# A decoder layer on one core: linear attention's state taken per 128 tokens, seven products over whole chunks, and other buffers for the first loads

## The chip, the cores and the metric

The kernel runs on one core of one Trainium2 chip. The time is the device time of one execution in microseconds (us): the median of 3 runs was 1633.13 us (1632.35 to 1633.36). The profile is of one further execution.

## What is computed

One layer of a hybrid decoder on 256 tokens of width 2048, with 256 memory tokens, all in float32. One wide projection of the normalised input feeds three branches: gated linear attention (4 heads, key width 128, value width 256), stick-breaking attention (8 heads of 128) and cross-attention into the memory (4 heads of 256). Each branch has its own projection to 2048, the three are merged by sigmoid gates, an output projection and a residual follow, then a SwiGLU block of inner width 5632.

```python
proj = rmsnorm(x, attn_norm) @ w_in     # gq gk gv gr ga1 | sq sk sv | mq | gates
log_a = log_sigmoid(ga1 @ gla_w_a2 + gla_b_a) / 16
# linear attention, per chunk of 64 tokens, b = cumsum(log_a) inside the chunk
q_e, k_e, k_d = q*exp(b), k*exp(-b), k*exp(b_last - b)
s = where(causal, q_e @ k_e.T, 0);   o = s @ v + q_e @ S
S = S * exp(b_last) + k_d.T @ v
...
merged = g0*y_gla + g1*y_sb + g2*y_mem
x = x + merged @ w_o
gate, up = split(rmsnorm(x, ffn_norm) @ w_gate_up)
x = x + (silu(gate) * up) @ w_down
```

## The kernel before

The 256 tokens are two halves of 128 rows (index `t`). Weights arrive from HBM as loads of 4 chunks of 128 rows by 512 columns (1 MB, tiles named `raw`). A float32 product is made of three matmuls in the type fp32r: each weight half-load (2 chunks, 128x1024) is split into a high and a low part (`wh` by a cast on ACT, L148; `wl` by a subtraction on DVE, L149), the activations were split once before, and high-high, high-low and low-high are added up in PSUM. Each such matmul streams 512 columns.

`gemm` (L221 to L223) multiplies all chunks by one block of 512 columns. `sgemm` (L262 to L265) takes two blocks at once and saves products: of the first 8 chunks, `p` chunks of each group of 4 are multiplied by seven products instead of eight (the scheme of Strassen in the form of Winograd: two token halves, two groups of chunks, two blocks). The sums of activations (`sh`, `sl`; `sd` for the last projection) are made once; the sums of weights are made on DVE in place (`raw<-raw`, L277) and by accumulating transfers that POOL issues (L319, L339). What is left of the chunks goes through `rest`, eight products as usual. `sgemm` begins with product `p1` into a temporary bank, which ACT copies into the accumulator (`acc<-tmp`, L302) before `rest` adds to it. With `late=True` it postpones the products that need the sums of activations. Its `put` keeps partial results in scratch pieces (`cv`).

Work on vectors and small matmuls runs in the background: generators in a list `background`; `gemm` and `sgemm` advance the first of them by one piece at each `step()` (after each half-load of a product or of `rest`), and `flush()` runs out what is left. Within that a planner orders the instructions of each engine; each engine then runs its own in that order and waits on semaphores.

The stages in time: memory keys and values (to about 99 us), the memory queries `mq` (to 145), `sq` with memory attention in the background (to 207), `sk`, `sv` (to 293), `gqk` and `gv` with the stick-breaking heads in the background (to 394), `gr`, the two branch projections with linear attention in the background (440 to 554), gates and the third branch (to 847), the output projection `w_o` in two pairs of blocks (to 935), and the SwiGLU block in three parts. The last down projection has 12 chunks; its first pair of blocks goes through `sgemm`, the last two blocks through `gemm`, and `stored` adds them to the residual (`x2s`, L1113) and sends them out.

Linear attention (`gla`, L820 to L905) takes each 128 tokens as two chunks of 64. The scores of both chunks are one matmul per head with a mask that keeps the two 64x64 diagonal blocks; the state `S` (128x256 per head) is used and renewed for each 64 tokens, with matmuls that use half the tokens (L883: `S` with 64 columns of queries; L888: 64 rows of keys and values). These are plain float32 matmuls, which the trace shows as two passes each.

At the start there are three `raw` tiles (`ring1`), and 8 matmuls on zeros run before the first weights are there (L564).

Of the kernel before, what the change touches and what calls it, by code (L numbers as in the profile page):

```python
# [59 lines left out]
def constants():  # L60
    i, j = np.arange(P)[:, None], np.arange(P)[None, :]
    same = (i // GC) == (j // GC)
    blocks = [
        i == j,
        i < j,
        (i <= j) & same,
        i > j,
        np.ones((P, P), bool),
        (i <= j) & same,
        (i > j) & same,  # L70
        (i // GC) == np.arange(P // GC)[None, :],
    ]
    scale = [1, 1, 1, 1, 1, 1 / TAU, 1 / TAU, 1 / TAU]
    return np.concatenate([b.astype(np.float32) * np.float32(s) for b, s in zip(blocks, scale)], 1)
# [3 lines left out]
def trunk(ctx: ExitStack, tc: tile.TileContext, a, out):  # L78
# [11 lines left out]
    def widen(name, raw, w, side="right"):  # L90

        pool = tc.alloc_tile_pool(name=name, bufs=1, side=side, reuse_waits="tile")
        free_raw.extend([(pool, raw)] * raw)
        splits.extend([(pool, w)] * w)
        return pool

    def narrow(pool):

        for x in (free_raw, splits):
            x[:] = [y for y in x if y[0] is not pool]  # L100
        pool.release()
# [70 lines left out]
    def loads():  # L172

        slot = pool, bufs = free_raw.pop(0)
        return pool.tile([P, KG, NB], F32, tag="raw", name="raw", bufs=bufs), lambda: free_raw.append(slot)
# [54 lines left out]
    def sgemm(xs, forms, w, blks, p, row0=0, late=False, moved=True):  # L230
# [62 lines left out]
        def put(at, *src):  # L293

            if late or at[0]:
                c[at] = piece()
                dst = c[at][:]
            else:
                dst = o[at][:]
                begun.add(id(o[at]))  # L300
            if len(src) == 1:
                act.copy(dst, src[0][:])  # L302
            else:
                dve.tensor_tensor(dst, src[0][:], src[1][:], op=ALU.subtract)
# [184 lines left out]
    def normed_T(dst, src, heads, dim, gain, scratch):  # L489


        ss = small.tile([P, 2, heads], F32, name="hn_ss")
        for t in range(2):
            for n in range(0, MIX, NB):
                sq = scratch()
                act.activation(sq[:], src[:, t, n : n + NB], AF.Square)
                dve.tensor_reduce(
                    ss[:, t, n // dim : (n + NB) // dim],
                    sq[:].rearrange("p (h d) -> p h d", d=dim),
                    axis=AX.X,  # L500
                    op=ALU.add,
                )
            yield
        y = rsqrt_mean(ss[:].rearrange("p t h -> p (t h)"), dim, 2 * heads)
        for t in range(2):
            v = src[:, t].rearrange("p (h d) -> p h d", h=heads)
            dve.tensor_tensor(
                v, v, y[:, t * heads : (t + 1) * heads].unsqueeze(2).to_broadcast([P, heads, dim]), op=ALU.mult
            )
            yield  # L510
        yield
        e = dim // P
        for c in range(0, 8, 2 * e):
            for q in range(e):

                p = tmp()
                for i in range(2):
                    ch = c + q + i * e
                    for t in range(2):
                        transpose(p[:, i * T + t * P : i * T + (t + 1) * P], src[:, t, ch * P : (ch + 1) * P])  # L520
                d = dst[:, c + q : c + q + e + 1 : e, :]
                act.activation(d, p[:].rearrange("p (c t) -> p c t", c=2), AF.Copy, scale=gain[:, q : q + 1])
                yield
# [29 lines left out]

    mk, mkT = section("mk", "a"), chunks(section("mkT", "b")[:])
# [8 lines left out]
    for _ in range(8):  # L563
        pe.matmul(idle[:], zeros[:, :P], zeros[:], start=True, stop=True)  # L564
# [47 lines left out]
    xs = [x() for x in xs]  # L612
    mempool.release()
# [111 lines left out]
    wide(sq, O_SQ)  # L725
    flush()
    skT_sv = main.tile([P, 2, 2, MIX], F32, tag="resid", name="skT_sv")
    skT, sv_ = chunks(skT_sv[:, 0]), skT_sv[:, 1]
    sqT = chunks(section("sqT", "b")[:])
    sk = section("sk", "d")  # L730
    background.append(normed_T(sqT, sq, SH, SD, g_sqs, ra))
    wide(sk, O_SK)
    flush()
    background.append(normed_T(skT, sk, SH, SD, g_sk, ra))
# [58 lines left out]
    wide(gqk, O_GQ, 2)  # L793
    wide(gv, O_GV, 2)
# [23 lines left out]
    def gla():  # L818
        for t in range(2):
# [15 lines left out]
            b, bl, dc = tmp(), tmp(), tmp()  # L835
            for dst, w in ((b, tri), (bl, rest)):
                pe.matmul(dst[:], w, lh[:], start=True, stop=False)
                pe.matmul(dst[:], w, ll[:], start=False, stop=True)
# [5 lines left out]
            qe, ke, kd = ra(), ra(), ra()  # L844
            act.activation(qe[:], b[:], AF.Exp)
            act.activation(ke[:], b[:], AF.Exp, scale=-1.0)
            act.activation(kd[:], bl[:], AF.Exp)
# [4 lines left out]
            dve.tensor_tensor(kd[:], gqk[:, t, 512:], kd[:], op=ALU.mult)  # L852
            yield from pause(3)
            turned = []
            for src in (qe, ke):
# [3 lines left out]
                turned.append(rb()[:].rearrange("p (h t) -> p h t", h=GH))  # L859
                dve.tensor_copy(turned[-1].rearrange("p h t -> p (h t)"), p[:])  # L860
                yield from pause(2)
            qeT, keT = turned
            yield from pause(2)
            p = tmp()
            for h in range(GH):
                pe.matmul(p[:, h * P : (h + 1) * P], keT[:, h], qeT[:, h], start=True, stop=True)
            sT = ra()[:].rearrange("p (h t) -> p h t", h=GH)
            nc.gpsimd.memset(sT, 0.0)
            dve.copy_predicated(sT, causal4, p[:].rearrange("p (h t) -> p h t", h=GH))
# [3 lines left out]
            o = [tmp(), tmp()]  # L873
            ov = [o[h // 2][:, h % 2 * GDV : (h % 2 + 1) * GDV] for h in range(GH)]
            vh = [gv[:, t, h * GDV : (h + 1) * GDV] for h in range(GH)]
            for c in range(2):
                s = slice(c * GC, (c + 1) * GC)
                for h in range(GH):
                    if c == 0:

                        pe.matmul(ov[h], sT[:, h], vh[h], start=h % 2 == 0, stop=False, skip_group_check=True)
                    if (t, c) != (0, 0):
                        pe.matmul(ov[h][s], qeT[:, h, s], S[h][:], start=False, stop=c == 1, skip_group_check=True)  # L883
                if (t, c) != (1, 1):
                    d = [tmp(), tmp()]
                    for h in range(GH):
                        dh = d[h // 2][:, h % 2 * GDV : (h % 2 + 1) * GDV]
                        pe.matmul(dh, kd[s, h * GDK : (h + 1) * GDK], vh[h][s], start=True, stop=True)  # L888
                        if (t, c) == (0, 0):
                            dve.tensor_copy(S[h][:], dh)  # L890
                        else:
                            f = dec[:, 2 * h + c : 2 * h + c + 1]
                            dve.scalar_tensor_tensor(S[h][:], S[h][:], f, dh, op0=ALU.mult, op1=ALU.add)
                    yield from pause(3)
# [154 lines left out]
    for n0 in range(0, D, 2 * NB):  # L1049
# [4 lines left out]
        for j, result in sgemm(ms, sm_, a["w_o"], (n0 // NB, n0 // NB + 1), 2, late=n0 == 0):  # L1054
# [28 lines left out]
    for part in (range(0, 4), range(4, 8), range(8, NF)):  # L1083
# [25 lines left out]
        def stored(n, result, width=NB):  # L1109
            for t in range(2):  # L1110
                for c in range(0, NB, width):
                    v = x2s[t][:, n + c : n + c + width]
                    dve.tensor_tensor(v, v, result(t)[:, c : c + width], op=ALU.add)  # L1113
                    nc.sync.dma_start(out[t * P : (t + 1) * P, n + c : n + c + width], v)

        for n0 in range(0, D, 2 * NB):
            if final and n0 > 0:
                for n in (n0, n0 + NB):
                    o = gemm(fs, a["w_down"], n, row0=4 * part[0])

                    stored(n, lambda t: o[t], NB // 2 if n + NB == D else NB)
                continue
            blks = (n0 // NB, n0 // NB + 1)
            for j, result in sgemm(fs, sd, a["w_down"], blks, 4, row0=4 * part[0], moved=False):
                n = n0 + j * NB
                if final:
                    stored(n, result)
                    continue
                for t in range(2):
                    v = piece()  # L1130
                    act.copy(v[:], result(t))
                    nc.gpsimd.dma_start(x2d[:, t, n : n + NB], v[:], accum_op=ALU.add)

# [50 lines left out]
```

## Time and profile before

| | |
|---|---|
| median of 3 runs | 1633.13 us |
| the profiled execution | 1632.16 us, span 1630.4 us |
| PE (matmuls) busy | 1620.5 us, 99% |
| PEld (weight loads into PE) busy | 1325.9 us, 81% |
| DVE busy | 1331.5 us, 82% |
| ACT busy | 1028.4 us, 63% |
| POOL busy | 71.2 us, 4% |
| read from HBM | 325.09 MB |
| granted TensorE clock | 1.00 |

The span runs from the first to the last instruction; the execution's own time is 1.8 us longer. PE's busy time is made of matmuls that overlap: one lasts 0.39 us from its start to its modelled end, while the next starts earlier, so work on PE is counted here by the distance of starts.

### The profile page before, as it was taken

How to read it: one execution, taken by the hardware profiler on the slowest of the kernel's cores; microseconds unless marked ns; L12 is line 12 of the kernel's file. 1: busy time of each engine (PE TensorE's matmuls, PEld its weight loads, DVE VectorE, ACT ScalarE, POOL GpSimd, SP SyncE). 2: the span in 40 equal slices, each digit the busy share in tenths (PEclk: the TensorE clock that was granted, in tenths of full speed). 3: DMA queues.
4: the chain of work that ended last, by engine and by line, in shares of the span. 5: the costliest groups of instructions: out<-in, count | busy, mean ns of one | idle time of the engine just before them, and what ended most of it. 6: DMA issues, size and time to landing. Idle time of an engine off the chain costs nothing.

```text
span 1630.4 us, 19473 instructions
## 1 busy us (share of the span) xinstructions
PE 1620.5 (99%) x7266; PEld 1325.9 (81%) x7266; DVE 1331.5 (82%) x1526; ACT 1028.4 (63%) x1251; POOL 71.2 (4%) x93
## 2 busy tenths in 40 slices
PE   9999999999999999999999999999999999999999
PEld 6888778888877788888888888888888888888887
DVE  6867788877755788897897798988888989888994
ACT  7765576766744666666565566666666666666662
POOL 0000000000000000000000000000110000110000
PEclk9999999999999999999999999999999999999999
DMA  8795667656654888888657768687897687897682
GB/s 328 281 326 161 216 223 247 201 178 203 210 166 165 283 263 257 265 281 301 185 215 234 257 225 265 207 278 245 255 281 243 208 268 255 264 263 246 203 331 92
DMA packets 65888, 390.33 MB, mean 239 GB/s; under 512 B 7265, under 2 KB 13921, under 8 KB 21633
## 3 DMA queue, kind: packets, MB, share of 16 engines
q1 hardware_dynamic: 51344, 324.36, 53.0%
q0 software_dynamic: 11504, 61.87, 19.7%
q10 hardware_dynamic: 2944, 2.85, 0.5%
q8 instruction: 57, 0.93, 0.2%
q14 instruction: 39, 0.31, 0.1%
HBM read 325.09 MB, written 12.58 MB: 207 GB/s over the span
## 4 chain that ended last, share of the span: by engine, by line
PE 96%; DMA 1%; ACT 1%; DVE 1%; issue 0%; ACTq 0%; DVEq 0%
PE acc L262 19%; PE acc L265 19%; PE acc L264 19%; PE acc L221 6%; PE acc L222 6%; PE acc L223 6%; PE tmp L262 6%; PE tmp L265 6%; PE tmp L264 6%; PE tmp L441 2%; ACT wh L148 1%; DMA raw<-in_w_mem_kv 0%; DMA od_mem<-out 0%; DVE wl L149 0%; PE tmp L888 0%; PE tmp L883 0%
## 5 line engine op out<-in xcount | busy, mean ns | idle before, releaser
L149 DVE TENSOR_TENSOR wl<-raw,wh 128x1024 fp32r<-128x1024 f32 (+1 forms) x752 | 904.2, 1220 | 240.0 <-ACT wh L148 227.1
L148 ACT CAST wh<-raw 128x1024 fp32r<-128x1024 f32 (+1 forms) x752 | 783.0, 1052 | 455.1 <-PE acc L265 239.3
L262 PE MATMUL acc<-wh,xTh 128*128 128x512 f32 x504 | 200.6, 399 | 1.7 <-ACT acc L302 1.5
L265 PE MATMUL acc<-wh,xTl 128*128 128x512 f32 x504 | 196.6, 390 | 0.0
L264 PE MATMUL acc<-wl,xTh 128*128 128x512 f32 x504 | 196.4, 390 | 0.0
L262 PE MATMUL acc<-wh,hh 128*128 128x512 f32 x452 | 178.9, 396 | 0.0
L264 PE MATMUL acc<-wl,hh 128*128 128x512 f32 x452 | 176.2, 390 | 0.0
L265 PE MATMUL acc<-wh,hl 128*128 128x512 f32 x452 | 175.1, 390 | 0.0
L277 DVE TENSOR_TENSOR raw<-raw 128x1024 f32<-128x1024 f32 x122 | 147.9, 1220 | 0.7
L221 PE MATMUL acc<-wh,oh 128*128 128x512 f32 x320 | 127.2, 399 | 0.7 <-ACT oh L151 0.6
L222 PE MATMUL acc<-wl,oh 128*128 128x512 f32 x320 | 126.0, 394 | 0.9 <-DVE wl L149 0.9
L223 PE MATMUL acc<-wh,ol 128*128 128x512 f32 x320 | 125.8, 393 | 0.0
L262 PEld LDWEIGHTS acc<-wh,xTh 128*128 128x128 f32 x504 | 94.6, 188 | 24.0 <-ACT acc L302 4.8
L265 PEld LDWEIGHTS acc<-wh,xTl 128*128 128x128 f32 x504 | 94.6, 188 | 20.1
L264 PEld LDWEIGHTS acc<-wl,xTh 128*128 128x128 f32 x504 | 94.7, 188 | 18.8
L262 PE MATMUL tmp<-wh,sh 128*128 128x512 f32 x270 | 106.5, 394 | 0.0
L265 PE MATMUL tmp<-wh,sl 128*128 128x512 f32 x270 | 105.4, 391 | 0.0
L264 PE MATMUL tmp<-wl,sh 128*128 128x512 f32 x270 | 105.3, 390 | 0.0
L262 PEld LDWEIGHTS acc<-wh,hh 128*128 128x128 f32 x452 | 84.9, 188 | 18.7 <-ACT acc L302 1.0
L265 PEld LDWEIGHTS acc<-wh,hl 128*128 128x128 f32 x452 | 84.9, 188 | 17.8
L264 PEld LDWEIGHTS acc<-wl,hh 128*128 128x128 f32 x452 | 85.0, 188 | 16.8
L221 PEld LDWEIGHTS acc<-wh,oh 128*128 128x128 f32 x320 | 60.6, 190 | 17.1 <-issue 3.2
(311 smaller groups left out, 2368.4 us busy)
## 6 DMA issues: line engine op xcount, KB each, us to landing
raw<-in_w_gate_up SPq DMA_DIRECT2D x88, 1024.0 KB, 6.1
raw<-in_w_in SPq DMA_DIRECT2D x56, 1024.0 KB, 5.1
raw<-in_w_gate SPq DMA_DIRECT2D x48, 1024.0 KB, 7.0
raw<-raw POOLq DMA_DIRECT2D x45, 1024.0 KB, 8.0
raw<-in_w_down SPq DMA_DIRECT2D x44, 1024.0 KB, 7.3
raw<-in_w_o SPq DMA_DIRECT2D x16, 1024.0 KB, 5.8
raw<-in_w_mem_kv SPq DMA_DIRECT2D x15, 1024.0 KB, 6.0
raw<-in_w_br_mem SPq DMA_DIRECT2D x8, 1024.0 KB, 5.1
```

The source lines that it names most:

```text
L148: act.copy(hi, src)
L149: dve.tensor_tensor(lo, src, hi.bitcast(F32), op=ALU.subtract)
L221: pe.matmul(o[t][:], xh[:, s], wh[:, j], start=k == 0, stop=False)
L222: pe.matmul(o[t][:], xh[:, s], wl[:, j], start=False, stop=False)
L223: pe.matmul(o[t][:], xl[:, s], wh[:, j], start=False, stop=k == nk - 1)
L262: pe.matmul(dst[:], xh, wh, start=id(dst) not in begun, stop=False, skip_group_check=True)
L264: pe.matmul(dst[:], xh, wl, start=False, stop=False, skip_group_check=True)
L265: pe.matmul(dst[:], xl, wh, start=False, stop=last, skip_group_check=True)
L277: dve.tensor_tensor(x, x, y, op=ALU.add)
L441: pe.transpose(dst, src, ident)
```

## The change

- `sgemm` uses the seven products on all 4 chunks of a group instead of 2 in `gqk`, `gv` and both pairs of `w_o` (`p` from 2 to 4; `SP` is 4). The last pair of the last down projection goes through `sgemm` with `p=2` and an order of its own (`end`) instead of two `gemm`. There, partial results of the second token half are added to the residual at once (`base`).
- Linear attention: cumulative sums, causal mask and state are taken over 128 tokens. The state is made once (from the first 128 tokens) and used once. To keep the exponents small, queries of the second 64 tokens are held in two forms, and the scores of those columns are made a second time with 64 columns. The state's four copies go from DVE to ACT, which also makes two copies of the queries per 128 tokens.
- The first loads may also use the tiles `sh`, `sl` and `d`, which are free at that time; 10 matmuls on zeros instead of 8.
- `normed_T` idles for 3 steps before it begins in three of its uses; the queries' normalisation of stick-breaking goes into the background of `sk` without a flush ahead of it.

```diff
-        (i <= j) & same,
+        i <= j,
...
-        (i > j) & same,
+        i > j,
...
-    for _ in range(8):
+    for _ in range(10):
         pe.matmul(idle[:], zeros[:, :P], zeros[:], start=True, stop=True)
...
+    free_raw.extend([(fpool, 1, "sh"), (fpool, 1, "sl"), (sec, 1, "d")])
...
+            if base and at[0]:
+                v = base(at[1])
+                dve.tensor_tensor(v, v, src[0][:], op=ALU.add)
+                if len(src) > 1:
+                    dve.tensor_tensor(v, v, src[1][:], op=ALU.subtract)
+                return
...
+        elif end:
+            seq = [a, *l21, *r0, g, h, *l22, b, *l11, e, *l12, i, f, *r1]
...
-    background.append(normed_T(mqT, mq, MH, MD, g_mq, ra))
+    background.append(normed_T(mqT, mq, MH, MD, g_mq, ra, 3))
...
+    def q_T():
+        sqT.append(chunks(section("sqT", "b")[:]))
+        yield from normed_T(sqT[0], sq, SH, SD, g_sqs, ra, 3)
+    background.append(q_T())
+    sk = section("sk", "d")
+    wide(sk, O_SK)
     flush()
...
-    wide(gqk, O_GQ, 2)
-    wide(gv, O_GV, 2)
+    wide(gqk, O_GQ)
+    wide(gv, O_GV)
...
-            b, bl, dc = tmp(), tmp(), tmp()
-            for dst, w in ((b, tri), (bl, rest)):
+            sums = [(tri, tmp())] + ([(rest, tmp())] if t == 0 else [])
...
+            act.copy(qT[:, :, :GC], p[:, :, :GC])
+            dve.tensor_tensor(qT[:, :, GC:], p[:, :, GC:], first_64, op=ALU.mult)
+            act.copy(q2, p[:, :, GC:])
...
+                pe.matmul(p2[:, h * GC : (h + 1) * GC], keT[:, h], q2[:, h], start=True, stop=True)
...
-                    if (t, c) != (0, 0):
-                        pe.matmul(ov[h][s], qeT[:, h, s], S[h][:], start=False, stop=c == 1, skip_group_check=True)
-                if (t, c) != (1, 1):
-                        pe.matmul(dh, kd[s, h * GDK : (h + 1) * GDK], vh[h][s], start=True, stop=True)
+                if t == 1:
+                    pe.matmul(ov[h], qT[:, h], S[h][:], start=False, stop=True, skip_group_check=True)
+            if t == 0:
+                    pe.matmul(d[h], kd[:, h * GDK : (h + 1) * GDK], vh[h], start=True, stop=True)
+                    act.copy(S[h][:], d[h])
...
-        for j, result in sgemm(ms, sm_, a["w_o"], (n0 // NB, n0 // NB + 1), 2, late=n0 == 0):
+        for j, result in sgemm(ms, sm_, a["w_o"], (n0 // NB, n0 // NB + 1), SP, late=n0 == 0):
...
-            if final and n0 > 0:
-                for n in (n0, n0 + NB):
-                    o = gemm(fs, a["w_down"], n, row0=4 * part[0])
...
+            end = final and n0 + 2 * NB == D
+            base = (lambda j: x2s[1][:, n0 + j * NB : n0 + (j + 1) * NB]) if final else None
+                fs, sd, a["w_down"], blks, 2 if end else SP, row0=4 * part[0], moved=end, base=base, end=end
```

Over the whole program PE has 30 fewer matmuls of 128x512 with weights, two fewer of that size in the cumulative sums, 16 fewer float32 matmuls of 256 columns and 8 more of 64 columns. ACT has 15 more casts `wh` of 128x1024, DVE 15 more subtractions `wl` and 11 more additions `raw<-raw` of that size.

The first place is PE in linear attention, first 128 tokens (`gv` are values, `ra` masked scores or keys, `S` the state, `rb` queries or keys). Before:

```order
L866 MATMUL tmp<-rb 128x128 x4
...
L881 MATMUL tmp<-gv,ra 128x256 x4
L888 MATMUL tmp<-gv,ra 128x256 x2
...
L883 MATMUL tmp<-S_3679,rb 64x256
L883 MATMUL tmp<-S_3680,rb 64x256
L883 MATMUL tmp<-S_3681,rb 64x256
L883 MATMUL tmp<-S_3682,rb 64x256
L888 MATMUL tmp<-gv,ra 128x256 x2
```

Now:

```order
L908 MATMUL tmp<-ra,rb 128x128 x4
L910 MATMUL tmp<-rb 128x64 x4
...
L928 MATMUL tmp<-gv,ra 128x256 x4
L934 MATMUL tmp<-gv,ra 128x256 x2
...
L934 MATMUL tmp<-gv,ra 128x256 x2
```

The products with the state (L883) are gone from this half, the state's renewal is there once instead of twice, and the second scores (L910) stand right behind the first.

The second place is ACT at the change from `sq` to `sk` (`ra<-sq` squares `sq` for its normalisation, `acc<-tmp` is the copy behind `p1`, `rb<-tmp` a transposed piece of memory attention). Before:

```order
L714 ACTIVATE sq<-acc,r_x 128x512
L496 ACTIVATE ra<-sq 128x512 x2
L148 CAST wh<-raw 128x1024
L714 ACTIVATE sq<-two,r_x 128x512
L148 CAST wh<-raw 128x1024
L496 ACTIVATE ra<-sq 128x512
L302 COPY acc<-tmp 128x512
```

Now:

```order
L734 ACTIVATE sq<-two,r_x 128x512
L664 COPY out<-tmp 128x256 x2
L665 DMA od_mem<-out 128x256 x2
L714 COPY rb<-tmp 128x512
L512 ACTIVATE ra<-sq 128x512 x2
L314 COPY acc<-tmp 128x512
```

Two squares and the last copy of memory attention stand ahead of the copy behind `p1`, where a cast and a square stood; the products of that last memory head now stand on PE between `p1` and the first `rest` of `sk`.

The third place is DVE in `gqk`, from the first values of the second stick-breaking head to its last (`rb<-tmp,ra`, `ra<-tmp,ra`, `rb<-rb,cst` and `rd<-rb,rc` make what the second small matmul of a head needs, `ra<-ra,tmp` and `ra<-ra,cst` what the third needs). Before:

```order
L767 SCALAR_TENSOR_TENSOR rb<-tmp,ra 128x384
L768 SCALAR_TENSOR_TENSOR ra<-tmp,ra 128x384
L769 TENSOR_TENSOR rb<-rb,cst 128x2x128
L149 TENSOR_TENSOR wl<-raw,wh 128x1024
L149 TENSOR_TENSOR rd<-rb,rc 128x384
L149 TENSOR_TENSOR wl<-raw,wh 128x1024
L779 TENSOR_TENSOR ra<-ra,tmp 128x384
L149 TENSOR_TENSOR wl<-raw,wh 128x1024
L781 TENSOR_TENSOR ra<-ra,cst 128x2x128
L304 TENSOR_TENSOR acc<-two,tmp 128x512
```

Now:

```order
L805 TENSOR_TENSOR ra<-ra,tmp 128x384
L793 SCALAR_TENSOR_TENSOR rb<-tmp,ra 128x384
L807 TENSOR_TENSOR ra<-ra,cst 128x2x128
L794 SCALAR_TENSOR_TENSOR ra<-tmp,ra 128x384
L795 TENSOR_TENSOR rb<-rb,cst 128x2x128
L152 TENSOR_TENSOR wl<-raw,wh 128x1024
L152 TENSOR_TENSOR rd<-rb,rc 128x384
L152 TENSOR_TENSOR wl<-raw,wh 128x1024
L805 TENSOR_TENSOR ra<-ra,tmp 128x384
```

The second head's values begin before the first head's last ones. On PE, between the first and the second small matmul of the first four heads there stood 24, 30, 30 and 36 matmuls with weights; now there stand 32, 22, 18 and 31. Between the second and the third stood 29, 24, 30 and 24 where now 12, 24, 15 and 13 stand.

More of the change, by code (lines that the diff above doesn't have):

```diff
@@ L228, in gemm, with sgemm @@
         return o
-    def sgemm(xs, forms, w, blks, p, row0=0, late=False, moved=True):
+    def sgemm(xs, forms, w, blks, p, row0=0, late=False, moved=True, base=None, end=False):
         nk = len(xs)
@@ L487, in project, with normed_T @@
             evac(dst[:, :, n : n + NB], gemm(xs, w, c0 + n), rstd)
-    def normed_T(dst, src, heads, dim, gain, scratch):
+    def normed_T(dst, src, heads, dim, gain, scratch, wait=0):
+        for _ in range(wait):
+            yield
         ss = small.tile([P, 2, heads], F32, name="hn_ss")
@@ L612, in trunk @@
     xs = [x() for x in xs]
+    give_up(fpool)
+    give_up(sec)
     mempool.release()
@@ L725, in trunk @@
     wide(sq, O_SQ)
+    sqT = []
+    def q_T():
[4 more added lines that the diff above has]
+    wide(sk, O_SK)
     flush()
+    sqT = sqT[0]
     skT_sv = main.tile([P, 2, 2, MIX], F32, tag="resid", name="skT_sv")
     skT, sv_ = chunks(skT_sv[:, 0]), skT_sv[:, 1]
[L729 to L734, printed above, removed]
+    background.append(normed_T(skT, sk, SH, SD, g_sk, ra, 3))
     wide(sv_, O_SV)
@@ L834, in gla @@
             yield from pause(4)
-            b, bl, dc = tmp(), tmp(), tmp()
-            for dst, w in ((b, tri), (bl, rest)):
+            sums = [(tri, tmp())] + ([(rest, tmp())] if t == 0 else [])
+            dc = tmp()
+            for w, dst in sums:
                 pe.matmul(dst[:], w, lh[:], start=True, stop=False)
@@ L851, in gla, with turned @@
             dve.tensor_tensor(ke[:], gqk[:, t, 512:], ke[:], op=ALU.mult)
-            dve.tensor_tensor(kd[:], gqk[:, t, 512:], kd[:], op=ALU.mult)
+            if t == 0:
+                kd = ra()
+                act.activation(kd[:], sums[1][1][:], AF.Exp)
+                dve.tensor_tensor(kd[:], gqk[:, t, 512:], kd[:], op=ALU.mult)
             yield from pause(3)
-            turned = []
-            for src in (qe, ke):
+            def turned(src):
                 p = tmp()
@@ L872, in gla, with pairs_of @@
             ss = small.tile([P, GH], F32, name="g_ss")
-            o = [tmp(), tmp()]
-            ov = [o[h // 2][:, h % 2 * GDV : (h % 2 + 1) * GDV] for h in range(GH)]
             vh = [gv[:, t, h * GDV : (h + 1) * GDV] for h in range(GH)]
-            for c in range(2):
-                s = slice(c * GC, (c + 1) * GC)
-                for h in range(GH):
-                    if c == 0:
-                        pe.matmul(ov[h], sT[:, h], vh[h], start=h % 2 == 0, stop=False, skip_group_check=True)
-                    if (t, c) != (0, 0):
-                        pe.matmul(ov[h][s], qeT[:, h, s], S[h][:], start=False, stop=c == 1, skip_group_check=True)
-                if (t, c) != (1, 1):
[L885 to L894, printed above, removed]
+            def pairs_of(into):
+                return [into[h // 2][:, h % 2 * GDV : (h % 2 + 1) * GDV] for h in range(GH)]
+            ov = pairs_of([tmp(), tmp()])
+            for h in range(GH):
+                pe.matmul(ov[h], sT[:, h], vh[h], start=h % 2 == 0, stop=t == 0, skip_group_check=True)
+                if t == 1:
+                    pe.matmul(ov[h], qT[:, h], S[h][:], start=False, stop=True, skip_group_check=True)
+            if t == 0:
+                d = pairs_of([tmp(), tmp()])
+                for h in range(GH):
+                    pe.matmul(d[h], kd[:, h * GDK : (h + 1) * GDK], vh[h], start=True, stop=True)
+                    act.copy(S[h][:], d[h])
+            yield from pause(3)
             for h in range(GH):
```

64 lines of the change are left out of this document (36 added, 28 removed).

## The prediction

> **What bounds the kernel now.** I read the page first: busy times, the slices, the chain that ended last.
>
> ```profile
> PE 1620.5 (99%) x7266; PEld 1325.9 (81%) x7266; DVE 1331.5 (82%) x1526; ACT 1028.4 (63%) x1251; POOL 71.2 (4%) x93
> PEclk9999999999999999999999999999999999999999
> PE 96%; DMA 1%; ACT 1%; DVE 1%; issue 0%; ACTq 0%; DVEq 0%
> ```
>
> PE is busy throughout, at full clock in every slice, and 96% of the chain is matmuls. Busy time alone would not prove that PE is full, since a matmul's 0.39 us overlaps the next one's. So I took the timeline of the last block, where nothing else runs: the first and the last of 43 matmuls.
>
> ```profile
> 1616.60 0.39 PE L223 MATMUL acc<-wh,fl 128*128 128x512 f32 x1
> ...
> 1626.12 0.39 PE L223 MATMUL acc<-wh,fl 128*128 128x512 f32 x1
> ```
>
> 42 steps in 9.52 us: a matmul of 512 columns costs 0.2267 us of PE's time. 7266 records in 1630 us make 0.224 us each on average, so PE takes nearly the whole program at this pace. The waits of PE by releaser confirm it:
>
> ```profile
> PE acc L262 <- ACT acc L302: 1.5, 2, 1.3
> PE tmp L701 <- ACT rb L694: 1.1, 1, 1.1
> ```
>
> These are the two largest behind the first microseconds, and they are below 2 us. So the time is PE's work: a removed matmul counts, as long as DVE and ACT keep up.
>
> A page of the Trainium skill speaks against this. Perfetto Trace Analysis, Identifying the Most-Contended Engine, says that matmul occupancy is no good measure, that the share of weight loads is one, and that the engine with the highest occupancy is to be improved first. By that DVE's 82% stands above PE's 81%, and a change that takes from PE and gives to DVE would gain nothing. The measured pace disagrees: the columns set it, not the weight load of 0.19 us. I keep the reading as a rival.
>
> **Seven products on whole chunks.** For the first 8 chunks a pair of blocks needs 84 matmuls with `p=4`, 90 with `p=2`, 96 with `gemm`. Four pairs go from 90 to 84 and the last down pair from 96 to 90: 30 matmuls less, 30 x 0.2267 = **6.8 us**. All lie in stages where PE is full (the first five rows below).
>
> The price is on DVE and ACT: per pair 3 more half-loads split and 2 more additions (3 in the first pair of `w_o`).
>
> ```profile
> L149 DVE TENSOR_TENSOR wl<-raw,wh 128x1024 fp32r<-128x1024 f32 (+1 forms) x752 | 904.2, 1220 | 240.0 <-ACT wh L148 227.1
> L277 DVE TENSOR_TENSOR raw<-raw 128x1024 f32<-128x1024 f32 x122 | 147.9, 1220 | 0.7
> L148 ACT CAST wh<-raw 128x1024 fp32r<-128x1024 f32 (+1 forms) x752 | 783.0, 1052 | 455.1 <-PE acc L265 239.3
> ```
>
> 26 x 1.22 = 31.7 us more on DVE in all, 15 x 1.05 = 15.8 on ACT. Does it fit? By stage (stretch, length, then busy PE, PEld, DVE, ACT, POOL):
>
> ```profile
> 293.00:344.00 51.00, 50.98 (x239) 42.77 (x240) 40.71 (x55) 35.76 (x54) 1.75 (x2) 1.00 0.61 195
> 344.00:394.00 50.00, 49.83 (x231) 41.44 (x230) 37.67 (x46) 33.14 (x47) 1.72 (x2) 1.00 0.62 189
> 847.50:891.50 44.00, 44.00 (x203) 36.42 (x203) 33.33 (x35) 23.91 (x28) 2.30 (x3) 1.00 0.61 210
> 891.50:935.00 43.50, 43.50 (x200) 35.66 (x199) 31.88 (x38) 26.67 (x38) 3.11 (x5) 1.00 0.78 265
> 1595.00:1611.00 16.00, 16.00 (x72) 13.23 (x72) 11.56 (x12) 6.05 (x6) 0.00 (x0) 1.00 0.16 63
> ...
> 935.00:982.00 47.00, 47.00 (x216) 38.88 (x216) 45.36 (x72) 31.38 (x44) 2.51 (x4) 1.00 0.63 215
> 1564.00:1595.00 31.00, 31.00 (x142) 25.56 (x141) 30.61 (x32) 22.01 (x24) 0.88 (x1) 1.00 0.83 282
> ```
>
> `gqk` becomes 40.7 + 6.1 = 46.8 of DVE in 51.0 - 1.4 = 49.6 of PE (94%), `gv` 43.8 in 48.6, `w_o` 40.6 in 42.6 and 38.0 in 42.1. The last two rows show DVE at 97% and 99% with PE fully busy, so this load alone need not stop PE. The last down pair has room: DVE is idle for more than half of the end.
>
> What does bear on PE is the chain of the stick-breaking heads, which now share 22 steps per pair instead of 19. For the second head:
>
> ```profile
> 302.13 0.38 PE L761 MATMUL tmp<-sqT,skT_sv 128*128 128x128 f32 x2
> 302.85 0.48 ACT L763 ACTIVATE ra<-tmp 128x384 f32<-128x384 f32 x1
> 307.05 0.55 DVE L149 TENSOR_TENSOR rd<-rb,rc 128x384 fp32r<-128x384 f32 x1
> 310.31 0.22 PE L778 MATMUL tmp<-rd,cr 128*128 128x128 f32 x1
> 312.29 0.42 DVE L781 TENSOR_TENSOR ra<-ra,cst 128x256 f32<-128x256 f32 x1
> ```
>
> From the first small matmul's end (302.5) to `rd` (307.6) the chain takes 5.1 us; PE came back only at 309.9. From the second's end (310.5) to 312.7 it is 2.2 us. In the new order the shortest stretches on PE are 18 matmuls (4.1 us, plus about 0.8 for a third small matmul) and 12 (2.7 us). That is about even with the chain, where 24 matmuls (5.4 us) were the least. One split of 1.22 us at the wrong place on DVE then shows on PE, and behind a waiting small matmul all weight matmuls stand still. Bounds: nothing, to 8 heads x 1.22 = 9.8 us. Nearest are the rows above, where PE did not wait; the planner spreads the heads unevenly, and I take **+1.5 us** here and +0.5 for `w_o` and the down pair: **+2.0**.
>
> **Linear attention.** Small float32 products on PE (the timeline groups passes, two per product):
>
> ```profile
> 447.12 0.62 PE L837 MATMUL tmp<-rc,cr 128*128 128x512 f32 x2
> 461.27 1.05 PE L866 MATMUL tmp<-rb 128*128 128x128 f32 x8
> 470.34 1.89 PE L881 MATMUL tmp<-gv,ra 128*128 128x256 f32 x8
> 472.16 1.13 PE L888 MATMUL tmp<-gv,ra 64*128 64x256 f32 x4
> 478.78 1.94 PE L883 MATMUL tmp<-S,rb 128*64 128x256 f32 x8
> ```
>
> Taking the last pass's 0.38 (0.27) off and dividing by the steps: L881 (1.89 - 0.38)/7 = 0.216 us a pass, L883 0.223, L888 0.25, L866 0.11. Half the rows or columns cost as much as all, so two halves joined save one. Removed: 24 passes of L883 (5.4 us), 24 of L888 (6.0), two cumulative sums at 0.23 (0.5). Added: 8 passes of state by queries (1.8), 8 of keys by values (2.0), 16 of 64 columns. Those the trace doesn't have; they lie between 0.055 (half of L866) and 0.11, and I take 0.11 (1.8), because L866's short pass already seems bound by something other than columns. Sum **-6.3 us**; with the pass at 0.216 throughout and at 0.055, -5.6 to -7.2. DVE loses 8 renewals of the state, so it has room; the chain of 128 tokens gets shorter by the second chunk. All this is hidden behind `gemm`'s matmuls as before.
>
> **The turn from `sq` to `sk`.** Two of PE's waits lie here.
>
> ```profile
> 194.92 2.68 ACTq L645 DMA_DIRECT2D od_mem<-out  x2
> 197.65 0.58 ACT L694 COPY rb<-tmp 128x512 f32<-128x512 f32 x1 [2.48 <-PE acc L265]
> ...
> 207.75 0.62 ACT L496 ACTIVATE ra<-sq 128x512 f32<-128x512 f32 x1
> 208.28 0.57 ACT L302 COPY acc<-tmp 128x512 f32<-128x512 f32 x1
> 208.91 0.50 PE L262 MATMUL acc<-wh,xTh 128*128 128x512 f32 x1 [1.33 <-ACT acc L302]
> ```
>
> The second (1.33 us) comes from `sq`'s squares ahead of the copy behind `p1`. In the new order two squares are still ahead, but PE has the last memory head's products (1.94 us in the row of L883's size) before it needs the copy: **-1.3**. The first (1.1) comes from an ACT queue that took 2.68 us to issue two transfers; that order stays, so nothing. Bounds: both gone (-2.4) or none (0). The idle steps of `normed_T` cost nothing while the 22 steps of a pair cover them.
>
> **The opening.**
>
> ```profile
> 0.00:20.00 20.00, 17.20 (x55) 11.11 (x56) 12.23 (x21) 13.73 (x24) 0.20 (x4) 1.00 0.92 337
> 3.10 1.60 SPq L455 DMA_DIRECT2D xraw<-in_memT  x2
> 1.19 3.59 PE L564 MATMUL tmp<-zeros 128*128 128x512 bf16 x8 [1.19 <-DVE zeros L561]
> 5.38 0.79 PE L221 MATMUL acc<-wh,oh 128*128 128x512 f32 x1 [0.60 <-ACT oh L151]
> 5.56 7.27 DMA raw<-in_w_mem_kv
> 15.22 0.50 PE acc L222
> ```
>
> PE's dense run begins at 15.22, behind a 1 MB load issued at 5.56, when the first of the three buffers came free. With six buffers it can go out when SP has issued the transfers ahead of it (3.10 + 1.60 = 4.70), 0.86 us earlier, but the transfers already keep the 16 engines busy for 92% of the first 20 us. I take **-0.3**; bounds -0.86 and 0. The two matmuls on zeros (0.43 us each by the row) fill the gap ahead of 5.38 and cost under 0.1. DMA: Bandwidth & Descriptors, Where 436 GB/s comes from, in the Trainium skill gives 435 GB/s for the 16 engines against 337 here; at that rate the opening could shorten by an estimated 2 us. The share of 0.92 says that these small packets already fill them.
>
> **Tail.** The last matmul starts at 1626.12; additions and the last transfer end the span 4.3 us later. Their shape stays.
>
> **Sum.** -6.8 - 6.3 - 1.3 - 0.3 + 2.0 = -12.7 us on the profiled 1632.16: 1619.5. The median of the runs lies 1.0 above the profiled execution: **1620.5 us**.
>
> **Rivals.** *The stick-breaking chain eats the gain* (slower). If DVE is late by one split at both waits of each of the 8 heads, that is 19.5 us against 14.7 of gain without my +2.0: about 1638. It decides from 1.8 us per head. For it: the 12 and 18 matmuls; against: DVE at 94%. 0.06. *Half of it arrives*: waits of about 6 us more than assumed, in linear attention (18 matmuls between copy and scores instead of 24) or in `w_o`, where the accumulating transfers of 1 MB take 8.0 us to land instead of 4.6: 1626.5. 0.14.
>
> ```profile
> raw<-raw POOLq DMA_DIRECT2D x45, 1024.0 KB, 8.0
> raw<-raw POOLq DMA_DIRECT2D x8, 512.0 KB, 4.6
> ```
>
> *More than I count*: no new waits, both old ones gone, the opening 0.8 shorter: -6.8 - 7.2 - 2.4 - 0.8 = -17.2, so 1616. 0.10. *PE was not the bound*: the matmuls give nothing and DVE's 31.7 us are added: 1665. 0.02, against the pace measured above. The Trainium skill's Perfetto Trace Analysis, as cited, points this way.
>
> **Numbers.** The forecast has 0.68. Without the two slower cases and the far ends of the others, 8 in 10 lie between 1615 and 1627. A measurement tells 0.2% (3.3 us, 1629.9) from no change: faster takes the forecast, the larger gain and most of the half gain, 0.91; within, 0.04; slower, from the first and the last rival, 0.05.
>
> **What will show it.** PE's starts stay 0.227 apart; L883 and L888's successors have 8 passes each; PE's waits grow only for small matmuls between 290 and 390; the wait for `acc` near 207 is gone; PE's share stays at 99%. Wrong would be: weight matmuls waiting for `wl` in `gqk` or `w_o`, a dense run that begins after 15.2, or an end later than 4.3 us behind the last matmul.

## The result, and the profile after

The changed kernel takes 1613.81 us (median of 4 runs, 1612.68 to 1614.12), the kernel before 1632.74 (4 runs beside it): a ratio of 0.9884, interval 0.9868 to 0.9899. The gain is 18.9 us where 12.6 were forecast, and the time lies 1.2 us below the lower end of the range. The profiled execution of the changed kernel took 1612.68 us (span 1610.9), 19.5 less than that of before.

The page of the changed kernel, in the rows that the prediction read first (busy time and instructions, granted clock, chain that ended last):

```profile
PE 1603.4 (100%) x7220; PEld 1317.3 (82%) x7220; DVE 1356.4 (84%) x1545; ACT 1044.8 (65%) x1274; POOL 73.0 (5%) x95
PEclk9999999999999999999999999999999999999999
PE 98%; DMA 1%; DVE 0%; ACT 0%; issue 0%; SPq 0%; DVEq 0%; ACTq 0%
```

PE is busier still, DVE has risen by 25 us, and the bound has not moved. The view of waits lists, from 560 us to the end, one wait of PE on another engine, and between 140 and 440 none:

```profile
PE tmp L268 <- ACT wh L151: 0.7, 1, 0.7
```

Both large waits of before are gone. The stages whose DVE load the prediction worked out (`gqk`, `gv`, the two `w_o` pairs, the first gate-up pair; columns as there):

```profile
289.00:341.00 52.00, 52.00 (x244) 42.51 (x243) 45.59 (x64) 39.03 (x62) 0.88 (x1) 1.00 0.67 217
341.00:388.00 47.00, 47.00 (x217) 39.00 (x216) 41.57 (x47) 34.56 (x47) 2.59 (x3) 1.00 0.75 231
834.00:876.00 42.00, 42.00 (x196) 34.73 (x195) 37.97 (x41) 26.43 (x32) 2.16 (x4) 1.00 0.70 232
876.00:917.50 41.50, 41.50 (x190) 34.19 (x189) 37.42 (x42) 28.26 (x41) 3.46 (x6) 1.00 0.88 287
917.00:963.00 46.00, 46.00 (x213) 38.03 (x212) 44.35 (x70) 31.00 (x44) 2.54 (x4) 1.00 0.68 237
```

PE is full in all of them. DVE stands at 88 to 90% in the first four and at 96% in the last.

**Where the time went.** Each stage has as many weight matmuls in both kernels, apart from the 30 that are gone. So a stage can be measured between the same two weight matmuls, by count, in both traces, from PE's starts:

| Stage (times of before) | before, us | after, us | difference |
|---|---|---|---|
| opening, to 16 | 10.64 | 10.06 | -0.57 |
| memory, `mq`, to 142 | 126.17 | 126.19 | +0.03 |
| `sq`, `sk`, `sv`, to 291 | 148.83 | 144.94 | -3.89 |
| `gqk`, to 344 | 53.19 | 53.24 | +0.05 |
| `gv`, to 394 | 49.79 | 47.30 | -2.50 |
| `gr`, to 436 | 44.11 | 44.42 | +0.31 |
| linear attention, to 560 | 122.10 | 111.83 | -10.27 |
| branches and gates, to 849 | 288.91 | 289.74 | +0.83 |
| `w_o`, to 936 | 87.04 | 84.31 | -2.72 |
| gate-up, down, to 1595 | 658.90 | 658.89 | -0.01 |
| last down pair | 31.05 | 30.17 | -0.88 |

The sum is -19.6. Linear attention gave 4 us more than the prediction's -6.3, and the turn (the third row) 2.6 more than its -1.3. The rows of the seven products (`gqk`, `gv`, `gr`, gates, `w_o`, last pair) add up to -4.9, which is what the prediction had for them with its waits (-6.8 + 2.0 = -4.8).

### The profile page after: what moved, and what is told of

Its sections match the earlier page's. It is cut to its first block, busy times and chain, and to the rows that moved or that the text cites. A ratio compares the mean times of both kernels' runs of the same rounds, so it can differ in the third digit from the quotient of the medians.

```text
span 1610.9 us, 19440 instructions
## 1 busy us (share of the span) xinstructions
PE 1603.4 (100%) x7220; PEld 1317.3 (82%) x7220; DVE 1356.4 (84%) x1545; ACT 1044.8 (65%) x1274; POOL 73.0 (5%) x95
## 4 chain that ended last, share of the span: by engine, by line
PE 98%; DMA 1%; DVE 0%; ACT 0%; issue 0%; SPq 0%; DVEq 0%; ACTq 0%
PE acc L268 19%; PE acc L271 19%; PE acc L270 19%; PE tmp L268 7%; PE tmp L270 7%; PE tmp L271 7%; PE acc L225 5%; PE acc L224 5%; PE acc L226 5%; PE tmp L455 2%; DMA raw<-in_w_mem_kv 0%; PE tmp L693 0%; PE tmp L721 0%; PE tmp L803 0%; DMA xraw<-in_memT 0%; PE tmp L786 0%
## 5 line engine op out<-in xcount | busy, mean ns | idle before, releaser
L152 DVE TENSOR_TENSOR wl<-raw,wh 128x1024 fp32r<-128x1024 f32 (+1 forms) x767 | 922.0, 1222 | 212.5 <-ACT wh L151 199.6
L151 ACT CAST wh<-raw 128x1024 fp32r<-128x1024 f32 (+1 forms) x767 | 798.8, 1052 | 434.5 <-PE acc L271 224.5
L268 PE MATMUL acc<-wh,xTh 128*128 128x512 f32 x480 | 190.4, 397 | 0.0
L270 PE MATMUL acc<-wl,xTh 128*128 128x512 f32 x480 | 187.2, 390 | 0.0
L271 PE MATMUL acc<-wh,xTl 128*128 128x512 f32 x480 | 186.9, 390 | 0.0
L283 DVE TENSOR_TENSOR raw<-raw 128x1024 f32<-128x1024 f32 x133 | 161.4, 1221 | 0.6
L268 PE MATMUL tmp<-wh,sh 128*128 128x512 f32 x294 | 115.9, 394 | 0.7 <-ACT wh L151 0.7
L271 PE MATMUL tmp<-wh,sl 128*128 128x512 f32 x294 | 114.8, 390 | 0.0
L270 PE MATMUL tmp<-wl,sh 128*128 128x512 f32 x294 | 114.6, 390 | 0.0
L268 PE MATMUL acc<-wh,fh 128*128 128x512 f32 x220 | 86.5, 394 | 0.0
```

Of the source, the lines that this page charges most:

```text
L151: act.copy(hi, src)
L152: dve.tensor_tensor(lo, src, hi.bitcast(F32), op=ALU.subtract)
L268: pe.matmul(dst[:], xh, wh, start=id(dst) not in begun, stop=False, skip_group_check=True)
L270: pe.matmul(dst[:], xh, wl, start=False, stop=False, skip_group_check=True)
L271: pe.matmul(dst[:], xl, wh, start=False, stop=last, skip_group_check=True)
L283: dve.tensor_tensor(x, x, y, op=ALU.add)
```

## Experiments

Two explanations were open. *Mis-sized terms*: linear attention and the turn were worth more in themselves. *Together*: the parts help one another, since an earlier stage shifts the waits of a later one. The first four kernels each take one part of the change alone; their text is the corresponding part of the diff shown above.

### Linear attention alone

```
+ sums = [(tri, tmp())] + ([(rest, tmp())] if t == 0 else [])
+ (whole-chunk scores, S x q and kd x v; the constants with them)
```

> The kernel before with only linear attention changed (state per 128 tokens). The prediction's own price is -6.3 us. Theory 'switch': the small products cost what the starts on PE say in the trace of before (21.9 us for 104 passes, against 12.6 us for 86 after the whole change, and 1.0 us less on the weight matmuls next to them), because every change to a tile of 64 rows or 64 columns and back holds PE up: -10 us, so about 1622.5. Rival 'together': the gain beyond 6.3 us came from the other parts (an earlier stage that shifts the waits of this one), and alone the change gives -6 to -7, so about 1626.

Measured: 1622.91 us against 1632.81, ratio 0.9936 (0.9923 to 0.9948), so -9.9. By stages -10.28 lies in linear attention, and each later stage stands within 0.05 us of before. The term was mis-sized; nothing came from the other parts.

### The turn alone

```
-background.append(normed_T(mqT, mq, MH, MD, g_mq, ra))
+background.append(normed_T(mqT, mq, MH, MD, g_mq, ra, 3))
 ...
+background.append(q_T())
 sk = section("sk", "d")
 wide(sk, O_SK)
 flush()
```

> The kernel before with only the turn from sq to sk changed (the queries' normalisation and transposes moved behind the first steps of sk, three idle steps ahead of each normalisation). The prediction's own price is -1.3 us (the wait for the copy behind p1 goes, the wait behind ACT's slow DMA issue stays). Theory 'both': both waits go, and the restarts of PE behind them (0.1 us each), together -3.9 us by the trace of the whole change, so about 1629. Rival: the slow DMA issue (2.68 us) comes at the same place whatever the order, and its loss in the whole change was a matter of when the loads ran: -1.3, about 1631.4.

Measured: 1628.78 us, ratio 0.9974 (0.9966 to 0.9983), -4.0. Theory "both" holds.

### The opening alone

```
+free_raw.extend([(fpool, 1, "sh"), (fpool, 1, "sl"), (sec, 1, "d")])
-for _ in range(8):
+for _ in range(10):
```

> The kernel before with only the opening changed (three more buffers for the first loads, ten matmuls on zeros instead of eight). Prediction -0.3; by the trace of the whole change -0.6 (the dense run begins 0.48 us earlier, as the 1 MB load is issued 0.69 us earlier); the estimate at 435 GB/s would be -2. Expected 1632.2.

Measured: 1632.64 against 1632.81, ratio 1.0002 (0.9993 to 1.0011). No gain can be measured. The 0.48 us by which the dense run began earlier in the two profiles is within what the opening does by itself: the 30th weight matmul starts between 15.4 and 18.2 us (mean 16.4) in the 8 profiled executions with the old opening and between 15.5 and 17.5 (mean 16.2) in the 7 with the new one.

### The 30 matmuls alone

```
-wide(gqk, O_GQ, 2)
-wide(gv, O_GV, 2)
+wide(gqk, O_GQ)
+wide(gv, O_GV)
 (w_o with SP for 2, the last down pair with end, as in the diff)
```

> The kernel before with only the 30 matmuls taken away (seven products in gqk, gv, two w_o pairs and the last down pair). The prediction's price is -6.8 by count and +2.0 for new waits, -4.8. Theory 'no new waits': by the trace of the whole change these stages lost 6.1 us, so -6.1, about 1626.6. Rival 'chain': without the other parts the stick-breaking heads stall as the prediction's +1.5 says, -4.8 or less, about 1628.

Measured: 1628.35, ratio 0.9974 (0.9962 to 0.9985), -4.5. There are new waits, as the prediction had it; but they stand elsewhere. `gqk` and `gv` together lost 2.45 us where the count says 2.72, so stick-breaking costs 0.27. The rest is +0.28 in `gr`, +0.92 in the branches and gates and +0.48 in the last pair, by the same stages. What the 0.28 in `gr` hangs on is open. Nearly all of the one in the gates is the wait for `wh` that the view shows in the changed kernel too, and DVE's timeline shows where it comes from. Before:

```profile
684.77 0.69 DVE L1022 TENSOR_TENSOR merged<-merged,cv 128x512 f32<-128x512 f32 x1
685.37 2.35 DVE L277 TENSOR_TENSOR raw<-raw 128x1024 f32<-128x1024 f32 x2
```

With the 30 matmuls gone:

```profile
684.87 1.22 DVE L280 TENSOR_TENSOR raw<-raw 128x1024 f32<-128x1024 f32 x1
686.00 1.22 DVE L149 TENSOR_TENSOR wl<-raw,wh 128x1024 fp32r<-128x1024 f32 x1
687.14 1.22 DVE L280 TENSOR_TENSOR raw<-raw 128x1024 f32<-128x1024 f32 x1
```

A split now stands between the two additions, so the second sum, and the cast that needs it, come later by one split of 1.22 us. PE has no more than part of that in hand and waits 0.7.

The four medians add up to -18.6 against -18.9 for the whole, so the parts are independent to within what the runs can tell.

### What linear attention's passes cost

The prediction's price per pass came from groups of four and eight in the first 128 tokens. In the second 128 tokens of before, where the products alternate, the timeline of PE reads:

```profile
519.54 0.59 PE L881 MATMUL tmp<-gv,ra 128*128 128x256 f32 x2
520.06 0.65 PE L883 MATMUL tmp<-S,rb 128*64 128x256 f32 x2
520.64 0.70 PE L881 MATMUL tmp<-gv,ra 128*128 128x256 f32 x2
521.27 0.65 PE L883 MATMUL tmp<-S,rb 128*64 128x256 f32 x2
```

From start to start two passes take 0.52, 0.58, 0.63 us; two at 0.216 would take 0.43. In the changed kernel the same pair of products, now both on a tile of 128 by 128:

```profile
502.39 0.59 PE L928 MATMUL tmp<-gv,ra 128*128 128x256 f32 x2
502.82 0.59 PE L930 MATMUL tmp<-S,ra 128*128 128x256 f32 x2
503.25 0.59 PE L928 MATMUL tmp<-gv,ra 128*128 128x256 f32 x2
503.68 0.59 PE L930 MATMUL tmp<-S,ra 128*128 128x256 f32 x2
```

0.43 us each. The suspicion is the column behind the names, the tile (the rows by columns of the array that the matmul uses): it goes from 128\*128 to 128\*64 or 64\*128 and back. To measure the price of such a change alone, 12 products of 64 rows were added to the changed kernel, once in a row and once one behind each of the 12 products with values or state (L928, L930). The added work is the same in both, and its results are not used.

```
+ def extra(h):
+     pe.matmul(d[h], sT[:GC, h], vh[h][:GC], start=True, stop=True, ...)
+ (in a row: extra(h) for all h ahead of the products;
+  between: extra(h) behind each product)
```

> The changed kernel with 12 extra products of 64 rows by 256 columns in linear attention (4 at the first 128 tokens, 8 at the second), each time all in a row ahead of the others; their results are overwritten or not read. 24 passes of 0.216 us are 5.2 us. Theory 'switch' (a change to a tile of 64 rows and back costs PE about 0.4 us a visit, read from the trace of before: 0.09 at the last pass before, 0.10 at the first pass, 0.09 at the last, 0.1 to 0.2 at the matmul behind): 2 visits, so +6.0 against the changed kernel, 1619.8. Rival 'no price for the shape': +5.2, 1619.0.

> The same 12 extra products, but one behind each of the 12 products of 128 rows (sT by values and queries by state), so that PE changes the shape of its tile 12 times there and back. Theory 'switch': 12 visits of 0.4 us, 5.2 + 4.8 = +10.0 against the changed kernel, and 4.0 more than the kernel with the products in a row: about 1623.8. Rival 'no price for the shape': same as in a row, 1619.0.

Measured against the 1613.8 us of the changed kernel: in a row 1619.60 (+5.8), between 1622.85 (+9.0). By stages, without the opening, it is +6.05 and +10.12 in linear attention, 0.85 us for 2 changes of tile there and back and 4.9 for 12: 0.41 to 0.43 a visit. The timeline with the products between:

```profile
461.74 0.70 PE L929 MATMUL tmp<-gv,ra 64*128 64x256 f32 x2
462.37 0.70 PE L933 MATMUL tmp<-gv,ra 128*128 128x256 f32 x2
463.00 0.70 PE L929 MATMUL tmp<-gv,ra 64*128 64x256 f32 x2
```

0.63 us from start to start on either side, 0.2 above two passes. The rival, no price for the shape, is out. The trace of before has 13 such visits in the products that the change rewrote, the changed kernel none. Passes at 0.216 and 0.11 alone give the -5.6 that stood as the prediction's near bound; the other 4.7 us are 0.36 for each of the 13. The added products have 64 rows; for a tile of 64 columns the evidence is the rows of before above. A page of the Trainium skill has the rule without a price: TensorEngine Tiling (Array Packing), Tiling Modes, says that a change of the tiling mode drains the engine. The rows above agree with it.

### The turn, in two pieces

```
 order alone:   ra, 3) -> ra) in all three calls of normed_T
 steps alone:   the order of before, and "3" in all three calls
```

> The kernel before with the new order of the turn, but no idle steps ahead of the normalisations. Theory 'order': the two waits went because the normalisation of sq's queries starts behind sk's first split and sk's loads; nearly all of the -4.0 us comes here, about 1629. Theory 'steps': the three idle steps did it; then this gives 0 to -1, about 1632.

> The kernel before with the old order of the turn and only the three idle steps ahead of each normalisation. Theory 'order': -1 at most (the squares come later than the copy behind p1, so the wait of 1.33 us may go), about 1632. Theory 'steps': -4, about 1629. What the two of this pair do to the issue that took ACT 2.26 us in every run of the old order (2.2 to 2.5) and 0.55 to 0.68 in the new one says what that hangs on: if it goes with the idle steps alone, then on the time between it and the 1 MB accumulating transfer that POOL issues 1.2 us earlier.

Measured: order alone 1632.76 (ratio 0.9993, 0.9984 to 1.0002), steps alone 1631.54 (0.9991, 0.9982 to 1.0000). Neither theory holds: each alone gives little or nothing (+0.2 and -0.1 us in the turn by stages), together they give 4.0. With the order alone, PE keeps both waits (1.7 and 0.9 us) and ACT's slow issue of 2.1 us. With the steps alone, the issue behind POOL's transfer takes 0.44 us and the wait for `acc` is gone. But the last memory head's product, which waited for `rb` in the old turn too, now waits longer, as the view of waits and the windows (columns as above) show:

```profile
PE tmp L703 <- ACT rb L696: 1.9, 1, 1.9
```

```profile
198.50:200.70 2.20, 0.28 (x3) 0.04 (x1) 0.27 (x1) 1.23 (x4) 0.00 (x0) 1.00 0.62 241
200.70:204.80 4.10, 4.09 (x11) 3.29 (x12) 3.55 (x7) 2.83 (x6) 0.00 (x0) 0.58 0.07 23
```

This wait has another cause. The product needs ACT's copy of its transposed weights right behind the transposes, because `flush()` drains the background at the end of the `sq` pair and no weight matmuls stand between. And behind that idle stretch PE's granted clock is 0.58 for 4.1 us: another 1.7 us. The steps remove the old loss and the old `flush()` makes a new one of the same size; moved behind `sk`, it lets `sk`'s matmuls cover the copy.

### What held ACT's issue

Each of the four memory heads sends out its result by a pair of transfers that ACT issues. In all kernels without the idle steps that keep POOL's transfer (the one before and five of the experiments), the second transfer of the third head takes 2.1 to 2.5 us to issue. POOL's transfer, a 1 MB addition between raw buffers, is issued shortly before. With the idle steps it is the second head's pair that comes next behind POOL; its second issue takes 0.44 or 0.45, and no other of these issues takes over 0.9. Before and after (POOL's row, then ACT's):

```profile
193.76 0.86 POOL L339 DMA_DIRECT2D raw<-raw  x1 [36.01 <-DVE ra L685]
```

```profile
188.81 0.86 POOL L351 DMA_DIRECT2D raw<-raw  x1 [31.53 <-DVE ra L705]
189.47 0.81 ACTq L665 DMA_DIRECT2D od_mem<-out  x2
```

In the changed kernel ACT's pair is issued 0.66 us behind POOL, before it was 1.16 (194.92, in the prediction's row), with the slow one of the pair 1.58 behind. In the changed kernel the second of the pair is 1.02 behind. Two kernels take an accumulating transfer away and let DVE add.

```
 if by_dma:
     nc.gpsimd.dma_start(q[22]..., q[12]..., accum_op=ALU.add)
+else:
+    for g in range(0, p, 2):
+        dve.tensor_tensor(x, x, y, op=ALU.add)   # x, y: halves of q[22], q[12]
```

> The kernel before, with the 1 MB addition between two raw buffers that POOL's queue carries out in the sq pair done by DVE instead (two additions of 1.22 us). Theory 'accumulating transfer': it is what held ACT's issue of the stores of o_mem for 2.2 us at 195.3, so the issue takes 0.33 to 0.45 us now and the wait of 1.1 us for rb goes; DVE's 2.4 us may show elsewhere; -1, about 1631.8. Rival: the issue is held by something else, stays at 2.2 us, and the time at 1632.8 or above.

This one (the `sq` pair) missed its aim: the transfer that it took away ran at 135.5 us, and the one near ACT's issue, of the `sk` pair, stayed. The issue stayed at 2.1 us, both waits stayed, the ratio is 0.9998 (0.9990 to 1.0007). So it told nothing of the theory, only that two additions on DVE cost nothing there. The next took the right one.

> The kernel before, with the 1 MB addition that POOL's queue carries out at 193.8 us (the sk pair's sixth product; the one taken from the sq pair ran at 135.5, far from the issue in question) done by DVE instead, two additions of 1.22 us. Theory 'accumulating transfer': ACT's issue at 195.3 takes 0.33 to 0.45 us instead of 2.1 to 2.5, the wait of 1.1 us of PE for rb goes, and the wait of 1.3 for acc stays: -1 less what DVE's additions hold up, 1631.8 to 1633. Rival: something else holds the issue; it stays at 2.1 us or more and the time does not fall.

Measured: 1629.22 us, ratio 0.9974 (0.9965 to 0.9983). ACT's pair is issued at the usual pace:

```profile
196.21 0.81 ACTq L650 DMA_DIRECT2D od_mem<-out  x2
```

and PE has neither of the two waits; the stage to 212 is 3.0 us shorter. More went than the theory had said: the wait for `acc` at 207, which the prediction put down to `sq`'s squares, went too, though the last square still stands right ahead of the copy:

```profile
205.99 0.62 ACT L501 ACTIVATE ra<-sq 128x512 f32<-128x512 f32 x1
206.51 0.57 ACT L302 COPY acc<-tmp 128x512 f32<-128x512 f32 x1
```

It was the same lateness of ACT, handed on along its queue. So the old turn's loss was one loss with one cause, the accumulating transfer beside ACT's issue. No run put a plain transfer of this size in its place, so the runs do not tell whether the adding, the size or POOL as the issuer matters. That the new turn escapes it by issuing 0.66 us behind POOL instead of 1.16 fits every trace here, but no run varied that distance alone.

### More of the same

Could the remaining half chunks go too? The changed kernel unedited was run beside them.

> The changed kernel once more, unedited, as the measure for the kernels beside it: 1613.8. Its stages behind the opening should repeat to within 0.1 us each; the opening should not.

```
-sgemm(hs, sf, a["w_gate_up"], (i, NF + i), 4 if i else 2, late=i == 0)
+sgemm(hs, sf, a["w_gate_up"], (i, NF + i), SP, late=i == 0)
```

> The changed kernel with seven products on whole chunks in the first pair of the gate-up projection too (the one pair of the feed-forward network that kept half chunks): 6 matmuls fewer, -1.36 us. Theory 'no new waits': 1612.4. Rival: DVE stands at 97% in this stage before the change, and 3 more split half-loads and 3 additions (7.3 us) do not fit; then PE waits for the splits and the gain is gone or turned round: 1613.8 to 1618.

```
-fs, sd, a["w_down"], blks, 2 if end else SP, ...
+fs, sd, a["w_down"], blks, SP, ...
```

> The same and whole chunks in the last down pair as well (96 to 84 matmuls instead of 90): 6 fewer again, where DVE is idle for half of the stage. -2.72 us in all if nothing waits: 1611.1. Rival: the end of the program keeps the later products' additions and stores behind the last matmul, so the tail grows by what is saved: 1612.4.

Measured: 1613.14 unedited, 1617.42 with the first gate-up pair, 1618.41 with the last down pair as well. Unedited, every stage but the opening and the turn (+0.53) repeated to within 0.1 us. With 6 matmuls fewer in the gate-up pair the kernel is 4.3 us slower. PE's waits between 900 and 1000 us, and the pair's stage:

```profile
PE acc L270 <- DVE wl L152: 1.6, 3, 0.7
PE tmp L270 <- DVE wl L152: 0.3, 1, 0.3
```

```profile
917.00:963.00 46.00, 44.01 (x197) 34.85 (x196) 45.82 (x71) 31.26 (x44) 2.54 (x4) 1.00 0.61 206
```

DVE is at 99.6% (45.82 of 46), PE at 95.7%: weight matmuls wait for `wl`. A further wait for DVE, 1.3 us, follows at 1010 us, behind the pair. This is the rival "PE was not the bound", in the one stage that had no room left. In the last pair PE waits 1.7 us for `wh`, whose casts wait for DVE's additions (3.9 us the longest), so more is lost than 6 matmuls save. Neither version is faster than the changed kernel.

## Why the prediction was wrong

**Direction and bound: right.** PE's starts stayed 0.2267 us apart, PE's share rose, and 30 matmuls gave what their count says wherever nothing new stood in the way (`w_o`: -2.72 for 12).

**Linear attention (-6.3): wrong in size; measured -9.9.** The step that failed is "L883 0.223, L888 0.25": I took the mean of passes in groups of four and eight at the first 128 tokens, and put the excess over 0.216 down to the pass. It was the change of tile, 0.36 to 0.43 us for each visit to a tile of 64 rows or columns. A price per visit weighs most on small groups: eight of the 13 visits lie in the second 128 tokens, six of them groups of two, and those I had not read. The added passes were right: the 64-column pass takes 0.11 (eight from 454.33 to 455.14 below, so 0.10 to 0.11 each), the others 0.216.

```profile
454.33 1.00 PE L910 MATMUL tmp<-rb 128*128 128x64 f32 x8
455.14 0.48 PE L224 MATMUL acc<-wh,oh 128*128 128x512 f32 x1
```

**The turn (-1.3): wrong; measured -4.0.** The step that failed is "that order stays, so nothing" for the wait behind ACT's issue. I had taken the 2.68 us as a property of the queue; it belonged to the moment, with POOL's transfer 1.16 us ahead. The other half, the second wait, came out as forecast, but for another reason: it was the same late ACT, not the squares. Even my bound "both gone (-2.4)" was too near, since it took the waits as the view lists them. The stages of the turn lost 3.5 us alone. Counted by starts, PE's gaps in the kernel before are 1.50 us (196.78 to 198.28) and 1.72 us (207.19 to 208.91) where a dense run has 0.23, so 2.8 us; where the rest lies is open.

**New waits (+2.0): right in the sum by luck, wrong in place.** The sum measured is +1.9 (seven products -4.9 by stages, -6.8 by count). Of that, stick-breaking has 0.27 instead of 1.5. `w_o` has none, the last pair 0.48, and 1.1 stand in `gr` and the gates, which I did not name. "PE's waits grow only for small matmuls between 290 and 390" was wrong: the view shows none there, and one at a weight matmul in the gates.

**Opening (-0.3): not measurable**, ratio 1.0002 alone. The estimate of 2 us at the 435 GB/s of the Trainium skill's page DMA: Bandwidth & Descriptors, Where 436 GB/s comes from, did not come, and the share of 0.92 that spoke against it was the better guide. In the kernel before, the share is 1.02 at 383 GB/s from 4 to 20 us; only the first 4 us, at 0.53 and 153 GB/s, have room.

**Tail: right.** The last matmul starts at 1606.58, 4.3 us ahead of the span's end.

**Rivals.** "More than I count" named the right direction, but would have got there by no new waits and 0.8 in the opening, neither of which held; what it gave the two terms (-7.2 and -2.4) was too small as well. The stick-breaking chain did not eat the gain: DVE at 88% in `gqk` absorbed the additions. That PE is not the bound was wrong for the program and right for the first gate-up pair, once 3 splits more are asked of it.

In numbers: linear attention 3.6 us and the turn 2.7 more than forecast, by the runs of the parts alone; together 6.3 us, as much as lies between 12.6 and 18.9. That this fits to a tenth is luck, since the medians of the parts are known to 1 or 2 us only; by the stages of the whole change it is 4.0 and 2.6.

## What to carry to other kernels

Count on PE not only passes but changes of the tile's shape: look at the tile column, and read the stretch where products alternate, not the one where they stand in a row. Where a wait hangs on an instruction that takes several times its usual length, ask what runs beside it at that moment, since moving either one frees it; and here the stage with DVE at 97% took no more splits, while the one at 80% took them for almost nothing. Single parts, run alone and compared stage by stage through PE's starts, told sizes to some tenths of a microsecond where medians told one or two.

## What the runs showed of the hardware

- **Tile shape.** A visit to a tile of 64 rows between tiles of 128 costs PE 0.41 to 0.43 us here, beside its passes of 0.216 each.
- **Clock behind a stall.** After 1.9 us of waiting PE ran 4.1 us at a granted clock of 0.58 (the row in the experiment on the steps alone); after the wait of 1.3 us at 207 in the kernel before it stayed at 1.00 (the window from 206 to 213):

```profile
206.00:213.00 7.00, 5.67 (x25) 4.35 (x25) 6.59 (x11) 4.89 (x7) 0.00 (x0) 1.00 0.09 14
```

  The length of the wait does not decide it alone. From start to start the first gap is 2.20 us and the second 1.72; the kernel with the new order alone has a gap of 2.09 at 207 and stays at 1.00. In the opening the clock falls in 5 of the 15 profiled executions, those with a gap of 1.77 us or more at 8 us. PE in the kernel with the 30 matmuls alone, and the window behind:

```profile
8.14 0.39 PE L223 MATMUL acc<-wh,ol 128*128 128x512 f32 x1
11.48 1.00 PE L221 MATMUL acc<-wh,oh 128*128 128x512 f32 x2 [2.95 <-ACT wh L148]
```

```profile
12.50:15.00 2.50, 2.26 (x5) 1.82 (x6) 1.76 (x5) 1.16 (x3) 0.00 (x0) 0.50 1.04 420
```

  The two matmuls behind the wait take 1.00 us, the clock in the window is 0.50, and the 30th weight matmul comes 1.5 us later than in the kernel before, whose opening this kernel has unedited. The Trainium skill's page TensorE: Matmul & The Clock Gate, Part 1, says that the clock falls back after an idle window of about 3.4 us; here a wait of 1.9 us was enough, and the measurement decides.
- **Issue beside an accumulating transfer.** An issue of ACT's took 2.1 to 2.5 us where a 1 MB accumulating transfer of POOL's had been issued 1.6 us before it, in six kernels out of six, and 0.39 with that transfer taken away. The others like it took 0.39 to 0.95 us. How the one holds the other is open.
- **The opening** varies by up to 2.8 us between executions (15.4 to 18.2 us to the 30th weight matmul), while in the unedited repeat the other stages agree to within 0.1 us, but for the turn (0.53). Over all runs a stage that an edit left alone differs by up to 0.6 us (memory and `mq` with the new order alone).
